# Experts in another order in the first block, and longer runs of weights per partition in the second

## The chip, the cores and the metric

The program runs on one core of a Trainium2 chip, with no other core at work. The metric is device time in microseconds (us) of one execution. Before the change the median of three runs is 2199.96 us, the lowest 2197.1 and the highest 2201.53. A profile comes from one further execution, whose own time is 2198.48 us.

## The reference

Everything is float32: 256 tokens of 1024 features go through two blocks.

The first block is `x + mixer(norm(x))`, then `x + memory_attention(norm(x))`, then `x + hierarchical_moe(norm(x))`. The mixture of experts there has 16 experts in four groups; each token takes two experts of one group:

```python
for e in range(16):
    act = silu(h @ w_gate[e]) * (h @ w_up[e])      # 1024 -> 256
    y = y + combine[:, e:e+1] * (act @ w_down[e])  # 256 -> 1024
```

The second block has two layers over 256 latent tokens and 256 context tokens. The first layer's mixer is a state space scan (SSD) in both directions, the second one's is attention. After each mixer comes an expert-choice mixture, in the first layer for latent and context tokens, in the last layer for latent tokens alone:

```python
gate, idx = top_k(softmax(h @ router_w).T, 32)     # 16 experts, 32 tokens each
xg = h[idx]
y = einsum(silu(xg @ w1[e]) * (xg @ w3[e]), w2[e]) # 1024 -> 1024 -> 1024
out.at[idx].add(y * gate)
```

`w1`, `w3` and `w2` are 4 MB for each expert, so 192 MB for each layer: they are most of what the program reads.

## The kernel before, in words

A tile here is a 128-partition buffer in SBUF. A TensorE instruction multiplies a stationary operand (`lhsT`, loaded by LDWEIGHTS, at most 128 x 128) with a moving one (`rhs`, up to 512 columns) into PSUM. SyncE (SP) issues every weight DMA, in its own program order, and none of them before the tile that it fills is free. A scheduler builds each engine's program from the order in which the Python code emits work and from a simulated timeline, so neighbouring instructions of one engine may come from different places in the code.

**The weight ring.** `ring()` hands out tiles of 128 x 4096 floats (2 MB) from a list of slots in turn: six in the first block's experts, seven in the first layer's of the second block, nine in its last layer's. A tile is refilled when every product that reads it is done.

**First block's experts** (`group_moe`, `group_round`). Tokens are put into expert slots, 64 for an expert, so a pair of experts has 128 rows. The one-hot matrix `oh` gathers: `gather` multiplies the token rows (`hi` and `lo`, two parts of the float32 value; the trace calls `hi` rhi and hT) with it, 32 matmuls for 512 slots, at line 1092, and evicts with the norm's gain `moe_norm_g` into `xg` at 1096 and 1098. `xg` is held as features on partitions: chunk k of eight has features 128k to 128k + 127. Then for each of eight pairs, in the order of the code: `oc` and its transposes (1107, 1111) and `back`, for the scatter; gate and up in one PSUM bank (1124), from two ring tiles, the upper and the lower 512 features of both experts; `act` (1136 to 1138) on ScalarE and VectorE; its transposes (1141) and `actT` (1143); the down product (1158) from one ring tile; `y` (1160, 1161); and the scatter into four accumulators (1165). `gate_order` names the tiles in the order of use; the first six are loaded ahead, while the mixer and the memory attention run.

The weights of that stage are laid out so that partition p has rows p, p + 128, ... of a matrix. A DMA of gate or up (1051) so has runs of 256 floats, 1 KB; one of down (1056) runs of 1024 floats, 4 KB.

**Second block's experts** (`choice_run`, `choice_group`). The first layer has 64 rows for each expert (32 latent, 32 context) and does groups of two experts, eight groups; the last layer has 32 rows and groups of four, four groups. A group does three products, `moe_w1_2`, `moe_w3_2` and `moe_w2_2`, each by `product` (1803): for each quarter q of the 1024 input features it takes one tile for each two experts and multiplies two chunks of features. Here partition p has features 8p to 8p + 7, next to each other in memory; a tile has two of these rows for each of two experts, and its two DMAs (`choice_tile`, 1653) have runs of 2 x 1024 floats, 8 KB. The gather of that stage (1765) already reads its stationary operand with a stride of eight, `v[:, i, k::8]`. A product's scatter is at 1851.

`group_round` is also built for later rounds, for tokens that didn't fit into the 64 slots; these parts are skipped when there are none, as in these runs.

Of the kernel before, what the change touches and what calls it, by code (L numbers as in the profile page):

```python
# [28 lines left out]
P = 128  # L29
D = 1024  # L30
T = 256
# [47 lines left out]
class Net:  # L79
# [861 lines left out]
    def group_moe(self, pool, tile_, late):  # L941
# [5 lines left out]
        nc.vector.tensor_tensor(wr, wr, self.colv("moe_norm_g")[:, :, None].to_broadcast([P, 8, 20]), op=OP.mult)  # L947
        self.hold = wr[:, 0, :1]
# [91 lines left out]
    gate_order = [x for i in range(8) for x in (("gu", i, 0), ("gu", i, 1), ("d", i, 0))]  # L1040

    def group_weights(self, what):

        kind, n, h = what
        a = self.a
        t = self.ring()
        if kind == "gu":
            v = t.rearrange("p (e k c) -> p e k c", e=2, k=4)
            for j in range(2):
                for m, nm in enumerate(("moe_w_gate", "moe_w_up")):  # L1050
                    self.nc.sync.dma_start(v[:, j, :, 256 * m:256 * m + 256],
                                           a[nm][0, 2 * n + j, 512 * h:512 * h + 512].rearrange("(k p) c -> p k c", p=P))
            return v
        v = t.rearrange("p (k c) -> p k c", k=4)
        for j in range(2):
            self.nc.sync.dma_start(v[:, 2 * j:2 * j + 2], a["moe_w_down"][0, 2 * n + j].rearrange("(k p) c -> p k c", p=P))
        return v

    def down_half(self, late, pr, n):

        w = late([P, 4, 512], "y", 2)
        for j in range(2):
            self.nc.sync.dma_start(w[:, 2 * j:2 * j + 2], self.a["moe_w_down"][0, 2 * pr + j][:, n * 512:(n + 1) * 512]
                                   .rearrange("(k p) c -> p k c", p=P))
        return w

    def group_round(self, r, ahead, tile_, late, hi, lo, pos, comb):
# [18 lines left out]
        g = self.colv("moe_norm_g")  # L1086
# [15 lines left out]
        for pr in range(E // 2):  # L1102
            if pr == 2:
                gather(1, "tf")
# [8 lines left out]
            junk = late([P, T], "act", 2)  # L1113
# [4 lines left out]
            if r == 0:  # L1118
                for h in range(2):
                    w = ahead.pop(0) if ahead else self.group_weights(("gu", pr, h))  # L1120
                    for k in range(4 * h, 4 * h + 4):
                        for j in range(2):
                            c0 = (2 * pr + j) * CAP
                            nc.tensor.matmul(gu[j * 64:j * 64 + 64], lhsT=xg[:, k, c0:c0 + CAP], rhs=w[:, j, k % 4],
                                             start=(k == 0), stop=(k == 7))
            else:
                for j in range(2):
                    c0 = (2 * pr + j) * CAP
                    for m, nm in enumerate(("moe_w_gate", "moe_w_up")):
                        w = late([P, 8, 256], "y", 2)  # L1130
                        nc.sync.dma_start(w, self.a[nm][0, 2 * pr + j].rearrange("(k p) c -> p k c", p=P))
# [656 lines left out]
    def choice_group(self, l, grp, EG, S, samples, xg, aff, pos, gr, actT, whole, tile_):  # L1788
# [5 lines left out]
        def product(nm, x):  # L1794
# [3 lines left out]
            for q in range(4):  # L1798
                ws = [self.choice_tile(nm, l, e0 + j, q) for j in range(0, EG, 2)]
                for k in (2 * q, 2 * q + 1):  # L1800
                    for n, p in enumerate(ps):
                        for j in range(EG):
                            nc.tensor.matmul(p[j * S:(j + 1) * S], lhsT=x(k, j),  # L1803
                                             rhs=ws[j // 2][:, j % 2, k % 2, n * 512:(n + 1) * 512],
# [332 lines left out]
```

## Time and profile before

| | |
|---|---|
| median of three runs | 2199.96 us (2197.1 to 2201.53) |
| the profiled execution | 2198.48 us, span of its instructions 2196.7 us |
| mean granted TensorE clock | 0.971 of full speed |
| busy TensorE, VectorE, ScalarE, GpSimd | 1960.7, 968.4, 633.2, 460.3 us |
| bytes moved | 603.53 MB, mean 275 GB/s |
| last of it, first block's experts | about 310 to 452 us |
| second block, first layer's experts | about 1057 to 1519 us |
| second block, last layer's experts | about 1741 to 2197 us |

The profile divides the span in 40 slices of 54.9 us; digits are busy tenths. A busy TensorE is not one at its peak: the ends of matmuls are modelled. The chain of waits goes back from the last instruction, at each step to what released it. The stages are told apart by the lines that run in them.

### The profile page before, as it was taken

How to read it: one execution, taken by the hardware profiler on the slowest of the kernel's cores; microseconds unless marked ns; L12 is line 12 of the kernel's file. 1: busy time of each engine (PE TensorE's matmuls, PEld its weight loads, DVE VectorE, ACT ScalarE, POOL GpSimd, SP SyncE). 2: the span in 40 equal slices, each digit the busy share in tenths (PEclk: the TensorE clock that was granted, in tenths of full speed). 3: DMA queues.
4: the chain of work that ended last, by engine and by line, in shares of the span. 5: the costliest groups of instructions: out<-in, count | busy, mean ns of one | idle time of the engine just before them, and what ended most of it. 6: DMA issues, size and time to landing. Idle time of an engine off the chain costs nothing.

```text
span 2196.7 us, 24031 instructions
## 1 busy us (share of the span) xinstructions
PE 1960.7 (89%) x9107; PEld 1043.9 (48%) x9128; DVE 968.4 (44%) x1643; ACT 633.2 (29%) x1174; POOL 460.3 (21%) x483
## 2 busy tenths in 40 slices
PE   7989879989999999889899999997989688888886
PEld 6667633356767777567333333333756322222211
DVE  6776542159777787666222222212765301010101
ACT  6554422154544555444100000001454200000000
POOL 4440110023233333522011111111753100000000
PEclk9999989999999999999999999999989899999998
DMA  7564949943232321275899999997538799999996
GB/s 243 184 205 135 304 169 346 324 155 107 87 106 69 123 87 54 93 248 205 331 420 419 420 420 419 420 419 311 221 125 312 285 421 420 421 420 421 421 421 280
DMA packets 185785, 603.53 MB, mean 275 GB/s; under 512 B 21555, under 2 KB 94982, under 8 KB 132414
## 3 DMA queue, kind: packets, MB, share of 16 engines
q1 hardware_dynamic: 185662, 601.92, 71.4%
q8 instruction: 74, 1.21, 0.2%
q14 instruction: 49, 0.40, 0.1%
HBM read 597.09 MB, written 4.78 MB: 274 GB/s over the span
## 4 chain that ended last, share of the span: by engine, by line
DMA 37%; PE 13%; DVE 3%; POOL 1%; ACT 1%; issue 1%; POOLq 0%; SPq 0%; DVEq 0%; ACTq 0%
DMA w<-in_moe_w_dram 37%; PE ps L1803 4%; PE ps L1765 1%; PE ps L1288 1%; PE ps L1287 1%; PE ps L1289 1%; PE ps L2024 1%; PE ps L2006 1%; POOL s L235 0%; PE ps L1220 0%; PE ps L1851 0%; PE ps L1698 0%; PE ps L1989 0%; DVE o L1854 0%; PE ps L1990 0%
## 5 line engine op out<-in xcount | busy, mean ns | idle before, releaser
L1803 PE MATMUL ps<-w,xg 128*64 128x512 f32 (+1 forms) x2048 | 497.2, 602 | 52.9 <-DMA w<-in_moe_w_dram 52.6
L1803 PEld LDWEIGHTS ps<-w,xg 128*64 128x64 f32 (+1 forms) x2048 | 142.5, 123 | 374.5 <-issue 242.5
L1855 POOL TENSOR_TENSOR x<-x,o 128x512 f32<-128x512 f32 x24 | 38.7, 1614 | 671.5 <-DVE o L1854 671.5
L1287 PE MATMUL ps<-hT,ws 128*128 128x512 f32 x384 | 156.7, 408 | 4.7 <-DVE ada L1222 4.5
L1288 PE MATMUL ps<-hT,ws 128*128 128x512 f32 x384 | 156.8, 408 | 0.0
L1289 PE MATMUL ps<-hT,ws 128*128 128x512 f32 x384 | 155.0, 404 | 0.0
L1803 PE MATMUL ps<-w,ctx 128*32 128x512 f32 x512 | 128.2, 599 | 23.8 <-DMA w<-in_moe_w_dram 22.7
L1803 PE MATMUL ps<-w,actT 128*64 128x512 f32 x512 | 129.3, 597 | 5.2 <-DMA w<-in_moe_w_dram 3.2
L1845 DVE SCALAR_TENSOR_TENSOR y<-ps,s,y 128x512 fp32r<-128x512 f32 x24 | 18.0, 748 | 261.5 <-ACT y L1844 261.5
L1493 DVE SCALAR_TENSOR_TENSOR conv<-pad,cols,conv 128x512 f32<-128x512 f32 x124 | 112.0, 904 | 2.6 <-ACT conv L1486 0.4
L1844 ACT ACTIVATE y<-ps,s 128x512 fp32r<-128x512 f32 x24 | 16.5, 686 | 327.1 <-PE ps L1803 260.5
L1287 PEld LDWEIGHTS ps<-hT,ws 128*128 128x128 f32 x384 | 72.6, 189 | 26.5 <-DVE ada L1222 5.2
L1803 PEld LDWEIGHTS ps<-w,ctx 128*32 128x32 f32 x512 | 29.2, 108 | 117.7 <-DMA w<-in_moe_w_dram 61.5
L1803 PEld LDWEIGHTS ps<-w,actT 128*64 128x64 f32 x512 | 45.3, 136 | 79.4 <-issue 64.4
L1288 PEld LDWEIGHTS ps<-hT,ws 128*128 128x128 f32 x384 | 72.7, 189 | 18.9 <-issue 3.8
L1289 PEld LDWEIGHTS ps<-hT,ws 128*128 128x128 f32 x384 | 72.6, 189 | 17.9 <-issue 1.9
L1282 DVE TENSOR_TENSOR ws<-wr,ws 128x1024 fp32r<-128x1024 f32 x48 | 62.3, 1299 | 41.3 <-ACT ws L1281 34.7
L1854 DVE TENSOR_TENSOR o<-ps,g 128x512 f32<-128x512 f32 x80 | 51.7, 686 | 62.2 <-PE ps L1851 61.7
L1282 DVE TENSOR_TENSOR ws<-w,ws 128x1024 fp32r<-128x1024 f32 x46 | 62.2, 1357 | 20.3 <-ACT ws L1281 19.9
L1555 POOL TENSOR_TENSOR seg<-seg,seg 128x512 f32<-128x512 f32 x32 | 47.1, 1471 | 114.4 <-ACT seg L1553 99.6
L1553 ACT ACTIVATE seg<-ps 128x512 f32<-128x512 f32 x96 | 54.7, 597 | 49.1 <-PE ps L1548 16.1
L1835 DVE TENSOR_TENSOR ctx<-ctx,ps 128x512 f32<-128x512 f32 x8 | 5.5, 687 | 140.1 <-PE ps L1803 140.1
(639 smaller groups left out, 3690.9 us busy)
## 6 DMA issues: line engine op xcount, KB each, us to landing
w<-in_moe_w_dram SPq DMA_DIRECT2D x384, 1024.0 KB
v<-in_ada_w_dram SPq DMA_DIRECT2D x32, 512.0 KB
w<-in_moe_w_up_dram SPq DMA_DIRECT2D x32, 512.0 KB
w<-in_moe_w_gate_dram SPq DMA_DIRECT2D x32, 512.0 KB
w<-in_moe_w_down_dram SPq DMA_DIRECT2D x16, 1024.0 KB
wr<-in_ssd_in_w_dram SPq DMA_DIRECT2D x16, 1024.0 KB
w<-in_ssd_out_w_dram SPq DMA_DIRECT2D x32, 512.0 KB
w<-in_ada_w_dram SPq DMA_DIRECT2D x8, 2048.0 KB
```

What stands on the lines that cost most here:

```text
L1282: (eng or self.nc.vector).tensor_tensor(lo, x, hi.bitcast(F32), op=OP.subtract)
L1287: t.matmul(p, lhsT=L[0], rhs=R[0], start=start, stop=False, **kw)
L1288: t.matmul(p, lhsT=L[0], rhs=R[1], start=False, stop=False, **kw)
L1289: t.matmul(p, lhsT=L[1], rhs=R[0], start=False, stop=stop, **kw)
L1493: nc.vector.scalar_tensor_tensor(seq(cv), pad[:, :, j:j + 256], tap(j), seq(cv), op0=OP.mult, op1=OP.add)
L1553: nc.scalar.activation(e, p, AF.Exp)
L1555: nc.gpsimd.tensor_tensor(ex[0][0], ex[0][0], ex[1][0], op=OP.add)
L1765: nc.tensor.matmul(p, lhsT=v[:, i, k::8], rhs=oh[:, i].rearrange("p e c -> p (e c)"), start=(j == 0), stop=(j == 3))
L1803: nc.tensor.matmul(p[j * S:(j + 1) * S], lhsT=x(k, j), rhs=ws[j // 2][:, j % 2, k % 2, n * 512:(n + 1) * 512], start=(k == 0), stop=(k == ...
L1854: nc.vector.tensor_tensor(o, q, gr[s][:, c], op=OP.mult)
L1855: (nc.gpsimd if i else nc.vector).tensor_tensor(xx[:, i, c], xx[:, i, c], o, op=OP.add)
L2006: nc.tensor.transpose(t[:, kt], L[:, par, kt * P:(kt + 1) * P], self.ident)
```

## The change

In the first block's experts the loop is split in two functions. `enter(pr)` has everything up to `act`; `leave(pr)` has the transposes of act, the down product and the scatter. `enter` of pair p + 1 now stands ahead of `leave` of pair p, and `gate_order` follows. The weights are laid out as in the second block: partition p has rows 8p to 8p + 7 of gate and up, and rows 2p and 2p + 1 of down, each next to each other in memory; a gate/up tile is one whole expert, with a run of 8 KB for gate and one for up, and down has runs of 8 KB. For that the gather reads `src[:, i, k::8]`, the transposes of act read `act[:, k::2]`, and the norm's gain is loaded a second time, as 8 for each partition (`moe_g`). A buffer of ScalarE's (`junk`) takes its space from another tag.

In the second block a product gets a parameter `nk`, the rows of one expert in a tile: with 2 a tile is as before; with 4 it is one expert's, filled by one DMA of 2 MB with runs of 16 KB. `nk` is 2 in the first and the last product of each layer and in the first layer's second product, and 4 in the other 21 of 24 and 10 of 12 products.

```diff
-    gate_order = [x for i in range(8) for x in (("gu", i, 0), ("gu", i, 1), ("d", i, 0))]
+    gate_order = [("gu", 0, 0), ("gu", 0, 1)] + [
+        x for i in range(8) for x in ([("gu", i + 1, 0), ("gu", i + 1, 1)] if i < 7 else []) + [("d", i, 0)]]
...
-            v = t.rearrange("p (e k c) -> p e k c", e=2, k=4)
-            for j in range(2):
-                for m, nm in enumerate(("moe_w_gate", "moe_w_up")):
-                    self.nc.sync.dma_start(v[:, j, :, 256 * m:256 * m + 256],
-                                           a[nm][0, 2 * n + j, 512 * h:512 * h + 512].rearrange("(k p) c -> p k c", p=P))
+            v = t.rearrange("p (m k c) -> p m k c", m=2, k=8)
+            for m, nm in enumerate(("moe_w_gate", "moe_w_up")):
+                self.nc.sync.dma_start(v[:, m], a[nm][0, 2 * n + j].rearrange("(p k) c -> p k c", k=8))
...
-                    nc.tensor.matmul(p, lhsT=src[:, i, k * P:(k + 1) * P], rhs=oh[:, i, n * 512:(n + 1) * 512],
+                    nc.tensor.matmul(p, lhsT=src[:, i, k::8], rhs=oh[:, i, n * 512:(n + 1) * 512],
...
-                for h in range(2):
-                    w = ahead.pop(0) if ahead else self.group_weights(("gu", pr, h))
-                    for k in range(4 * h, 4 * h + 4):
-                        for j in range(2):
-                            c0 = (2 * pr + j) * CAP
-                            nc.tensor.matmul(gu[j * 64:j * 64 + 64], lhsT=xg[:, k, c0:c0 + CAP], rhs=w[:, j, k % 4],
-                                             start=(k == 0), stop=(k == 7))
+                w = [ahead.pop(0) if ahead else self.group_weights(("gu", pr, j)) for j in range(2)]
+                for k in range(8):
+                    for j in range(2):
+                        c0 = (2 * pr + j) * CAP
+                        nc.tensor.matmul(gu[j * 64:j * 64 + 64].rearrange("p (m c) -> p m c", m=2),
+                                         lhsT=xg[:, k, c0:c0 + CAP], rhs=w[j][:, :, k], start=(k == 0), stop=(k == 7))
...
+            return act, back, ws
+
+        def leave(pr, act, back, ws):
...
-                nc.tensor.transpose(t[:, k], act[:, k * P:(k + 1) * P], self.ident)
+                nc.tensor.transpose(t[:, k], act[:, k::2], self.ident)
...
+        held = enter(0)
+        for pr in range(E // 2):
+            now = held
+            if pr == 2:
+                gather(1, "tf")
+            if pr + 1 < E // 2:
+                held = enter(pr + 1)
+            leave(pr, *now)
...
-    def choice_tile(self, nm, l, e0, q):
-
-        v = self.ring().rearrange("p (e k c) -> p e k c", e=2, k=2)
-        for e in range(2):
+    def choice_tile(self, nm, l, e0, nk, q):
+
+        v = self.ring().rearrange("p (e k c) -> p e k c", k=nk, c=D)
+        for e in range(4 // nk):
             src = self.a[nm][l, e0 + e].rearrange("(p k) c -> p k c", k=8)
-            self.nc.sync.dma_start(v[:, e], src[:, 2 * q:2 * q + 2])
+            self.nc.sync.dma_start(v[:, e], src[:, nk * q:nk * q + nk])
...
-            for q in range(4):
-                ws = [self.choice_tile(nm, l, e0 + j, q) for j in range(0, EG, 2)]
-                for k in (2 * q, 2 * q + 1):
+            ne = 4 // nk
+            for q in range(8 // nk):
+                ws = [self.choice_tile(nm, l, e0 + j, nk, q) for j in range(0, EG, ne)]
+                for k in range(nk * q, nk * q + nk):
...
+        for act, p in zip(acts, product("moe_w1_2", rows, 4 if grp else 2)):
...
+        for n, p in enumerate(product("moe_w3_2", rows, 4 if grp or EG > 2 else 2)):
...
+        for n, p in enumerate(product("moe_w2_2", lambda k, j: actT[:, k, j * S:(j + 1) * S], 4 if e0 + EG < 16 else 2)):
```

TensorE in the middle of the first block's experts, from the end of one pair's gate/up (L1124) over the transposes of act (L1141) and of oc (L1111) and the down product (L1158) to the first scatter (L1165). Before:

```order
L1124 MATMUL ps_6085<-w_6099,xg_5708 64x512 x4
L1141 MATMUL ps_6116<-const,act_6112 128x128 x2
L1111 MATMUL ps_6149<-const,oc_6147 128x128 x2
L1158 MATMUL ps_6125<-w_6121,actT_6119 64x512 x4
L1158 MATMUL ps_6132<-w_6121,actT_6119 64x512 x4
L1165 MATMUL ps_5761<-y_6124,back_6083 128x512
...
L1124 MATMUL ps_6157<-w_6158,xg_5708 64x512 x8
```

The same place now; gate/up is L1124 still, the transposes are L1145 and L1112, the down product L1162 and the scatter L1169:

```order
L1124 MATMUL ps_6108<-w_6112,xg_5702 64x512
L1124 MATMUL ps_6108<-w_6109,xg_5702 64x512
L1124 MATMUL ps_6108<-w_6112,xg_5702 64x512
L1162 MATMUL ps_6144<-w_6140,actT_6138 64x512 x4
L1162 MATMUL ps_6151<-w_6140,actT_6138 64x512 x4
L1145 MATMUL ps_6203<-const,act_6131 128x128 x2
L1112 MATMUL ps_6236<-const,oc_6234 128x128 x2
L1169 MATMUL ps_5755<-y_6143,back_6038 128x512
```

The down product stood behind the transposes of its own pair's act; now it stands ahead of them, and the act (act_6131) that is transposed behind it is the next pair's. Gate/up alternates between two tiles, and both are read to the end.

SP in the same stage, the DMAs for gate/up (L1051) and down (L1056) of a pair behind the first six tiles. Before:

```order
L1051 DMA w_5942<-in_moe_w_gate_dram 128x4x256
L1051 DMA w_5942<-in_moe_w_up_dram 128x4x256
L1051 DMA w_5942<-in_moe_w_gate_dram 128x4x256
L1051 DMA w_5942<-in_moe_w_up_dram 128x4x256
L1051 DMA w_5955<-in_moe_w_gate_dram 128x4x256
L1051 DMA w_5955<-in_moe_w_up_dram 128x4x256
L1051 DMA w_5955<-in_moe_w_gate_dram 128x4x256
L1051 DMA w_5955<-in_moe_w_up_dram 128x4x256
L1056 DMA w_5977<-in_moe_w_down_dram 128x2x1024 x2
L1051 DMA w_6014<-in_moe_w_gate_dram 128x4x256
```

The same now (gate/up L1054, down L1058):

```order
L1054 DMA w_5860<-in_moe_w_gate_dram 128x2048
L1054 DMA w_5860<-in_moe_w_up_dram 128x2048
L1058 DMA w_5888<-in_moe_w_down_dram 128x2048 x2
L1054 DMA w_5973<-in_moe_w_gate_dram 128x2048
L1054 DMA w_5973<-in_moe_w_up_dram 128x2048
L1054 DMA w_5976<-in_moe_w_gate_dram 128x2048
L1054 DMA w_5976<-in_moe_w_up_dram 128x2048
L1058 DMA w_6004<-in_moe_w_down_dram 128x2048 x2
L1054 DMA w_6041<-in_moe_w_gate_dram 128x2048
```

A gate/up tile had four DMAs of 128 x 4 runs of 256 floats; it has two with one run of 2048 floats for each partition. Behind the first gate/up tile there is now a down tile, then two gate/up tiles and a down tile in turn.

TensorE in the last layer of the second block, one product of four experts (ctx is the stationary operand, one for each expert). Before:

```order
L1803 MATMUL ps_15322<-w_15324,ctx 32x512 x2
L1803 MATMUL ps_15323<-w_15324,ctx 32x512 x2
L1821 MATMUL ps_15451<-const,oc_15442 128x128 x2
L1803 MATMUL ps_15322<-w_15327,ctx 32x512
L1803 MATMUL ps_15323<-w_15327,ctx 32x512
L1803 MATMUL ps_15322<-w_15327,ctx 32x512
L1803 MATMUL ps_15323<-w_15327,ctx 32x512
L1803 MATMUL ps_15322<-w_15324,ctx 32x512 x2
L1803 MATMUL ps_15322<-w_15327,ctx 32x512 x2
```

The same now (L1818; L1836 are transposes for the scatter):

```order
L1818 MATMUL ps_14865<-w_14867,ctx 32x512
L1818 MATMUL ps_14866<-w_14867,ctx 32x512
L1836 MATMUL ps_14986<-const,oc_14977 128x128 x2
L1818 MATMUL ps_14865<-w_14869,ctx 32x512
L1818 MATMUL ps_14866<-w_14869,ctx 32x512
L1818 MATMUL ps_14865<-w_14871,ctx 32x512
L1818 MATMUL ps_14866<-w_14871,ctx 32x512
L1818 MATMUL ps_14865<-w_14873,ctx 32x512
L1818 MATMUL ps_14866<-w_14873,ctx 32x512
L1818 MATMUL ps_14865<-w_14867,ctx 32x512
```

Two tiles of two experts each were read, several matmuls of one in a row; now four tiles of one expert each are read side by side, each to its fourth row.

## Rows read from the trace of the kernel before

**Rows 1.** The page: span, busy tenths of TensorE and DMA, bytes, in 40 slices.

```profile
span 2196.7 us, 24031 instructions
...
PE   7989879989999999889899999997989688888886
...
DMA  7564949943232321275899999997538799999996
GB/s 243 184 205 135 304 169 346 324 155 107 87 106 69 123 87 54 93 248 205 331 420 419 420 420 419 420 419 311 221 125 312 285 421 420 421 420 421 421 421 280
```

**Rows 2.** The page: the chain that ended last, by engine and by line.

```profile
DMA 37%; PE 13%; DVE 3%; POOL 1%; ACT 1%; issue 1%; POOLq 0%; SPq 0%; DVEq 0%; ACTq 0%
DMA w<-in_moe_w_dram 37%; PE ps L1803 4%; PE ps L1765 1%; PE ps L1288 1%; PE ps L1287 1%; PE ps L1289 1%; PE ps L2024 1%; PE ps L2006 1%; POOL s L235 0%; PE ps L1220 0%; PE ps L1851 0%; PE ps L1698 0%; PE ps L1989 0%; DVE o L1854 0%; PE ps L1990 0%
```

**Rows 3.** The chain in order of time: start us, us, what.

```profile
1100.17 13.95 PE ps L1803 x64
...
1257.99 19.94 DMA w<-in_moe_w_dram
...
2177.21 2.78 PE ps L1803 x18
```

**Rows 4.** TensorE in order of time, first block: start, us, what, [idle before <-releaser].

```profile
398.02 0.44 PE L1141 MATMUL ps<-const,act 128*128 128x128 f32 x2 [1.40 <-DVE act L1138]
398.94 3.65 PE L1158 MATMUL ps<-w,actT 128*64 128x512 f32 x16 [0.25 <-ACT actT L1143]
...
414.31 3.65 PE L1158 MATMUL ps<-w,actT 128*64 128x512 f32 x16 [0.25 <-ACT actT L1143]
```

**Rows 5.** Waits, 300 to 460 us: engine, what <- releaser: us, times, longest.

```profile
PE ps L1141 <- DVE act L1138: 11.6, 8, 1.8
...
PE ps L1158 <- ACT actT L1143: 2.0, 7, 0.5
```

**Rows 6.** Instructions of the two gathers, by line: ns minimum/median/maximum.

```profile
L1092 PEld LDWEIGHTS ps<-hT,rhi x32: 186/188/330, 310.0 to 357.9; 128*128 128x128 f32 x32
...
L1765 PEld LDWEIGHTS ps<-oh,hi x48: 312/329/342, 1018.9 to 1743.7; 128*128 128x128 f32 x48
```

**Rows 7.** TensorE in order of time where gather matmuls stand among others.

```profile
318.33 0.50 PE L1092 MATMUL ps<-hT,rhi 128*128 128x512 f32 x1
...
319.45 1.08 PE L1124 MATMUL ps<-w,xg 128*64 128x512 f32 x4
...
1730.66 0.63 PE L1765 MATMUL ps<-oh,hi 128*128 128x512 f32 x1
...
1731.96 1.92 PE L1803 MATMUL ps<-w,xg 128*32 128x512 f32 x16
```

**Rows 8.** SP in order of time, first block's experts.

```profile
330.50 1.42 SPq L1051 DMA_DIRECT2D w<-in_moe_w_up_dram  x1
...
388.23 2.11 SPq L1056 DMA_DIRECT2D w<-in_moe_w_down_dram  x2
```

**Rows 9.** Stretches: PE, PEld, DVE, ACT, POOL busy, clock, DMA share, GB/s.

```profile
330.00:335.00 5.00, 4.74 (x23) 1.78 (x21) 1.10 (x3) 2.12 (x5) 0.61 (x1) 1.00 1.09 348
394.00:398.00 4.00, 2.63 (x12) 0.77 (x10) 0.84 (x2) 0.38 (x1) 0.00 (x0) 1.00 1.03 407
1200.00:1250.00 50.00, 48.92 (x200) 19.11 (x197) 14.06 (x27) 4.34 (x8) 7.08 (x5) 1.00 1.01 421
```

**Rows 10.** The page: DMA packets by size; the instruction queue.

```profile
DMA packets 185785, 603.53 MB, mean 275 GB/s; under 512 B 21555, under 2 KB 94982, under 8 KB 132414
...
q8 instruction: 74, 1.21, 0.2%
```

**Rows 11.** TensorE in order of time, last layer of the second block.

```profile
1864.63 1.91 PE L1803 MATMUL ps<-w,xg 128*32 128x512 f32 x4 [0.60 <-DMA w<-in_moe_w_dram]
1867.12 4.39 PE L1803 MATMUL ps<-w,xg 128*32 128x512 f32 x24 [0.59 <-DMA w<-in_moe_w_dram]
```

**Rows 12.** A stretch at that layer's start (columns as in rows 9).

```profile
1760.00:1765.00 5.00, 4.90 (x15) 1.27 (x19) 0.00 (x0) 0.00 (x0) 0.00 (x0) 0.50 1.01 421
```

More of the change, by code (lines that the diff above doesn't have):

```diff
@@ L947, in group_moe @@
         nc.vector.tensor_tensor(wr, wr, self.colv("moe_norm_g")[:, :, None].to_broadcast([P, 8, 20]), op=OP.mult)
+        self.moe_g = tile_([P, 8], "g")
+        nc.sync.dma_start(self.moe_g, a["moe_norm_g"][0].rearrange("(p k) -> p k", k=8))
         self.hold = wr[:, 0, :1]
@@ L1038, in group_moe @@
         self.group_round(0, self.ahead, *env)
-    gate_order = [x for i in range(8) for x in (("gu", i, 0), ("gu", i, 1), ("d", i, 0))]
+    gate_order = [("gu", 0, 0), ("gu", 0, 1)] + [
+        x for i in range(8) for x in ([("gu", i + 1, 0), ("gu", i + 1, 1)] if i < 7 else []) + [("d", i, 0)]]
     def group_weights(self, what):
-        kind, n, h = what
+        kind, n, j = what
         a = self.a
@@ L1055, in group_weights @@
         for j in range(2):
-            self.nc.sync.dma_start(v[:, 2 * j:2 * j + 2], a["moe_w_down"][0, 2 * n + j].rearrange("(k p) c -> p k c", p=P))
+            self.nc.sync.dma_start(v[:, 2 * j:2 * j + 2], a["moe_w_down"][0, 2 * n + j].rearrange("(p k) c -> p k c", k=2))
         return v
@@ L1063, in down_half @@
             self.nc.sync.dma_start(w[:, 2 * j:2 * j + 2], self.a["moe_w_down"][0, 2 * pr + j][:, n * 512:(n + 1) * 512]
-                                   .rearrange("(k p) c -> p k c", p=P))
+                                   .rearrange("(p k) c -> p k c", k=2))
         return w
@@ L1085, in group_round @@
                 nc.vector.tensor_tensor(o, self.c("iota")[:, None, :].to_broadcast([P, E // 2, CAP]), wide(pr_), op=OP.is_equal)
-        g = self.colv("moe_norm_g")
+        g = self.moe_g
         def gather(n, tags):
@@ L1101, in group_round, with enter @@
         acc = [[self.ps(t) for t in "al"] for _ in range(2)]
-        for pr in range(E // 2):
-            if pr == 2:
-                gather(1, "tf")
+        def enter(pr):
             oc = tile_([P, 2, 2, CAP], "oc", 2)
@@ L1112, in group_round @@
             ws = self.st([P, 1])
-            junk = late([P, T], "act", 2)
+            junk = late([P, 2, P], "actT", 2).rearrange("p a q -> p (a q)")
             nc.scalar.activation(junk, t, AF.Copy, scale=0.5, accum_out=ws)
@@ L1130, in group_round @@
                         w = late([P, 8, 256], "y", 2)
[L1131 removed]
+                        nc.sync.dma_start(w, self.a[nm][0, 2 * pr + j].rearrange("(p k) c -> p k c", k=8))
                         for k in range(8):
@@ L1792, in choice_group, with product @@
         e0 = grp * EG
-        def product(nm, x):
+        def product(nm, x, nk=4):
             tag = self.turn("py")
             ps = [self.ps(tag) for _ in range(2)]
-            for q in range(4):
-                ws = [self.choice_tile(nm, l, e0 + j, q) for j in range(0, EG, 2)]
-                for k in (2 * q, 2 * q + 1):
+            ne = 4 // nk
+            for q in range(8 // nk):
+                ws = [self.choice_tile(nm, l, e0 + j, nk, q) for j in range(0, EG, ne)]
+                for k in range(nk * q, nk * q + nk):
                     for n, p in enumerate(ps):
@@ L1829, in choice_group @@
         rows = lambda k, j: xg[:, k, e0 + j].rearrange("p s c -> p (s c)")
-        for act, p in zip(acts, product("moe_w1_2", rows)):
+        for act, p in zip(acts, product("moe_w1_2", rows, 4 if grp else 2)):
             nc.scalar.activation(act, p, AF.Tanh, scale=0.5)
             nc.vector.scalar_tensor_tensor(act, act, 1.0, p, op0=OP.add, op1=OP.mult)
-        for n, p in enumerate(product("moe_w3_2", rows)):
+        for n, p in enumerate(product("moe_w3_2", rows, 4 if grp or EG > 2 else 2)):
             act = acts[n]
@@ L1841, in choice_group @@
             nc.scalar.activation(actT[:, 4 * n:4 * n + 4], t, AF.Copy)
-        for n, p in enumerate(product("moe_w2_2", lambda k, j: actT[:, k, j * S:(j + 1) * S])):
+        for n, p in enumerate(product("moe_w2_2", lambda k, j: actT[:, k, j * S:(j + 1) * S], 4 if e0 + EG < 16 else 2)):
             y = tile_([P, 2, 512], "y", 1, F32R)
```

2 lines of the change are left out of this document (1 added, 1 removed).

## The prediction

> **What bounds the kernel now.** I read the page first: its slices, then the chain of waits, then the chain in order of time, and only then single stages. In the slices [rows 1] two plateaus stand out, slices 21 to 27 and 33 to 39, where the DMA engines are full and move 419 to 421 GB/s. These are the two layers of experts of the second block. The chain of waits [rows 2] says the same: 37% of the span, some 810 us, is DMA into the weight tiles of these layers. In order of time [rows 3] the chain there is one link after another of 19.94 us for eight DMAs of 1 MB, which is 8.39 MB / 19.94 us = 420.7 GB/s. In the same rows TensorE does a whole product of the first layer (64 instructions) in 13.95 us when it has nothing to wait for, and a product's weights take 19.94 us: DMA is the bound, with 6 us to spare on TensorE. At the end DMA stops at 2177.2, and 19.5 us of products, scatter and norm follow.
>
> The first block's experts are another stage. In the steady state a pair of experts takes 15.37 us of TensorE from one down product to the next [rows 4]; in each, TensorE stands 1.40 us before the transposes of act and 0.25 us before the down product. Over the stage these are 11.6 and 2.0 us [rows 5]. No wait of TensorE for a weight DMA of any size is among them: TensorE bounds there, with DMA close behind.
>
> The sum is made against the profiled execution, 2198.5 us (span 2196.7 and 1.8 around it), which is 1.5 us under the median of the runs, 2199.96.
>
> **First block's experts, the order.** Before, TensorE did gate/up of a pair, waited for its act, transposed it, did its down product. Now the down product of pair p stands between gate/up of pair p+1 and the transposes of pair p+1. The down product takes 3.65 us [rows 4], the act chain 1.40 us: the wait is hidden, and likewise the 0.25 us for actT, behind the scatter. The second half of the down product writes the PSUM buffer from which act of p+1 is still read; its first half (1.8 us) covers these 1.40 us. Removed: 11.6 + 2.0 = 13.6 us. If the cover goes, because gate/up weights are late, the same 1.7 us per pair come back.
>
> Added: the gather and the transposes read their stationary operand with a stride. A contiguous load of the gather takes 188 ns, the strided one of the second block 329 ns [rows 6]. Where four gather matmuls stand between expert matmuls they take 319.45 - 318.33 = 1.12 us contiguous, and 1731.96 - 1730.66 = 1.30 us strided [rows 7]: 0.18 us a group, 2.9 us for 16 groups, nothing where loads run under other matmuls. Sixteen transposes of act with 0.14 us more each at most: 2.2 us. Bounds 0 and 5.1, taken 3. The small DMA of the gains goes out with the router's weights, some 20 us before the gather needs it: nothing.
>
> Weights of this stage: SP's rows tell what is in flight [rows 8]: gate and up in runs of 1 KB move 348 GB/s, down in runs of 4 KB 407 [rows 9]. A pair is 4.19 MB and 2.10 MB: 12.0 + 5.2 = 17.2 us of DMA; in runs of 8 KB at 420.7 it is 15.0 us. TensorE needs 15.37 - 1.65 = 13.7 us a pair from now on, so DMA would be next to bind, if six tiles (two pairs) were not loaded ahead. Both gate/up tiles of pair 0 are now freed together, when its gate/up products end and not half-way; from then DMA has 18 tiles of 4.98 us to bring, 90 us, and TensorE still has seven pairs of 13.7, the second gather (32 x 0.28 = 9 us) and a down product with its scatter, some 110 us. DMA ends early and stays hidden. The stage gains 13.6 - 3 = 10.6 by this; I take 9, since the first release comes later and y may be waited for at the end. Bounds: 14 and nothing. What follows up to the second block's experts is TensorE at nine tenths and more [rows 1], so a shift passes through.
>
> **Second block's weights.** Of 24 products of the first layer 21, and of 12 products of the second 10, get runs of 16 KB. At one link of 19.94 us for a product of two experts, and two for one of four, these are 21 x 19.94 + 10 x 39.88 = 817.5 us of DMA. No row has a 16 KB run on this queue. The time of a packet on one of 16 engines (16 x size / rate) is 47.1 ns for 1 KB, 161.0 for 4 KB, 311.5 for 8 KB [rows 3, 9]. Carried on from 4 and 8 KB (37.6 ns per KB) a 16 KB packet takes 612 ns, carried on from 1 and 8 KB 614: 427 to 428 GB/s, 1.5 to 1.7% less time, 12.2 to 13.9 us. I take 12, next to the row of 8 KB. The ends: all of the fixed part gone, 37.8 ns per KB or 434 GB/s, gives 25 us; cut into 8 KB again, 0, against which the instruction queue's 74 packets for 1.21 MB speak, 16 KB each [rows 10]; and, below nothing, a fall back to the 407 of 4 KB would cost 27 us, for which no row speaks, as each longer run here was faster.
>
> The Trainium skill ("DMA: Bandwidth & Descriptors", section "Why small descriptors are slow (HBM only)") gives a packet a fixed cost of about 3 cycles beside one per 32 bytes. By it 16 KB instead of 8 KB saves 3 of 518 cycles, 0.58%, 4.7 us in place of 12. By the same rule and its ceiling of 435 GB/s, runs of 1 KB would move 398 GB/s, and the trace has 348, so it disagrees on the size of the fixed cost.
>
> Tiles are now one expert's: a batch is two of them in the first layer, four in the second, and all come free together. In the second layer TensorE now does the first matmuls of each tile as it lands, and the rest after the fourth. Before, 24 instructions after the last landing took 4.39 us [rows 11]; the 52 now take at most 9.5. Five of nine slots are being filled meanwhile, 5 x 4.98 = 24.9 us of DMA, so SP has something to issue throughout. In the first layer it is two of seven slots, the same five, against 7 us of products. The first product of each layer and the last keep two rows, so start and end stay: no change of the 19.5 us.
>
> Sum: 2198.5 - 9 - 12 = 2177.5; on the scale of the median, 2179.
>
> **Rivals.** (B) Runs of 16 KB move no faster: DMA already stands at 420.7, and from 4 to 8 KB it gained 3% only. For it: no row of this queue above 8 KB. Against: the nearly straight line of the three packet times. Only the order gains: 2191.
> (C) The gain levels off: half or less of 12 us, because the fixed part is smaller at long runs. 2199.96 - 9 - 5 = 2186. It is also where the skill's 3 cycles lead, with its 4.7 us.
> (E) The first block gives nothing: DMA, at 15.0 us a pair against 13.7, takes over early, or the strided loads and the late first release eat the stalls. Against: the count of 90 to 110 us. 2200 - 12 = 2188.
> (D) Slower: TensorE loses its clock in the first layer. It now stands still for a tile's landing between short bursts. After such a stand the granted clock was 0.50 [rows 12], which is 1.2 GHz, and 15 instructions filled 4.9 us. A batch of 7 us has to fit DMA's 9.8. If the first half of each ran at 1.2 GHz it would take 10.5, 42 batches 440 us instead of 419: 21 lost there, 6 and 9 still won: 2206. It decides from a mean clock of 7.0 / 9.8 = 0.71. Against: from 1200 to 1250 TensorE did 200 instructions [rows 9], 43.6 us' worth at 13.95 / 64, so it stood for the rest, and the clock was 1.00; and a TensorE that is late has no gaps.
> The Trainium skill ("TensorE: Matmul & The Clock Gate", section "HAM oscillation — how this bites in real kernels") describes this: a kernel that waits for DMA before each slice starts each at the low clock. Rows 12 agree that a stand lowers it; rows 9 show that short ones did not.
>
> **How the numbers follow.** Forecast 0.62, B 0.11, C 0.10, E 0.08, D 0.09. The forecast's own range is 2168 to 2190: the stage 0 to 14, the runs 8 to 16. To hold 8 of 10 I take 2165 to 2194, which takes in B, C and E and leaves out D and a gain near the upper ends. A measurement of this kernel can tell about 0.2%, 4.4 us, from no change: faster is below 2195.6. D's chance is slower; of B, C and E a part falls within it: faster 0.83, same 0.08, slower 0.09.
>
> **What would show it.** In the profile after: the plateaus' GB/s at 427 or so, links of about 19.65 us for 8.39 MB, and some 21,000 packets fewer of 8 KB and more (512 for each of the 21 products, 1024 for each of the 10); waits of the transposes of act for act near nothing and about 13.7 us a pair; no SP wait between DMAs inside the plateaus. I am wrong if GB/s stays at 421, if TensorE waits for gate/up weights in the first block, if the first layer's plateau shows DMA below full, or if its clock falls below 1.

## The result and the profile after

The changed kernel takes 2186.28 us, median of four runs (2183.75 to 2188.18), where the kernel before takes 2200.74 (four runs, one more than above): a ratio of 0.9927, 95% interval 0.9913 to 0.9941, 14.5 us faster. The forecast was 2179 (2165 to 2194), 21 us faster. The direction held, and the size is two thirds of what was forecast. The profiled execution took 2188.18 us, its span is 10.3 us shorter than that of before.

The page of the changed kernel, the lines that answer to [rows 1, 10], with the granted clock:

```profile
span 2186.4 us, 23839 instructions
...
PE   7989879989999999889799898997989767667666
...
PEclk9999989999999999999899999999899889899989
DMA  7554748853232321275799999997537799999996
GB/s 243 179 191 148 294 171 327 365 166 97 87 107 62 127 92 54 88 237 199 317 428 426 426 427 426 428 427 308 223 126 288 288 428 426 429 427 428 427 425 278
DMA packets 131078, 603.49 MB, mean 276 GB/s; under 512 B 18563, under 2 KB 59222, under 8 KB 92558
```

The two plateaus (slices 21 to 27 and 33 to 39) now move 425 to 429 GB/s in place of 419 to 421, and there are 54,700 packets fewer. In slices 33 to 39, the last layer, TensorE's clock is at eight or nine tenths. The same in two stretches of the plateaus of the changed kernel (columns as in [rows 9]), and below them the second of these stretches before:

```profile
1200.00:1250.00 50.00, 47.10 (x196) 17.88 (x193) 14.15 (x27) 4.34 (x8) 7.08 (x5) 1.00 1.01 427
1800.00:2000.00 200.00, 136.49 (x674) 34.12 (x670) 17.65 (x32) 7.17 (x14) 6.46 (x4) 0.91 1.01 427
```

```profile
1800.00:2000.00 200.00, 170.68 (x672) 41.46 (x671) 17.68 (x32) 7.17 (x14) 6.18 (x4) 1.00 1.01 421
```

427 GB/s in both; in the last layer with a clock of 0.91 for TensorE, where it was 1.00. In the first block's experts, TensorE of the changed kernel in order of time, as in [rows 4]:

```profile
392.06 4.02 PE L1162 MATMUL ps<-w,actT 128*64 128x512 f32 x15
396.02 0.50 PE L1145 MATMUL ps<-const,act 128*128 128x128 f32 x2
...
406.22 4.02 PE L1162 MATMUL ps<-w,actT 128*64 128x512 f32 x15
410.17 0.50 PE L1145 MATMUL ps<-const,act 128*128 128x128 f32 x2
```

From one down product (L1162) to the next it is 14.16 us where it was 15.37, and the transposes of act (L1145) carry no wait in brackets. Of the waits of that stage, against [rows 5], one line is left:

```profile
PE ps L1162 <- ACT actT L1147: 0.3, 1, 0.3
```

At the end nothing changed (chain in order of time, as in [rows 3]):

```profile
2166.69 2.78 PE ps L1818 x18
```

Cut by instructions of TensorE, the stages of before and of the changed kernel in three executions (the other two from the runs e4 and g3 below) are, in us:

| | before | changed | e4 | g3 |
|---|---|---|---|---|
| start to the first gather of the first block's experts | 310.0 | 314.5 | 311.9 | 308.7 |
| first gather to the last scatter: first block's experts | 142.2 | 133.5 | 133.4 | 132.3 |
| to the first expert product of the first layer (SSD) | 605.6 | 608.1 | 607.5 | 606.5 |
| first to last product of the first layer | 464.8 | 460.0 | 460.0 | 460.0 |
| to the first read of keys in the attention | 74.9 | 77.9 | 78.2 | 77.2 |
| to the first expert product of the last layer | 131.2 | 130.7 | 130.8 | 131.0 |
| first to last product of the last layer | 452.0 | 445.6 | 445.5 | 445.7 |
| span | 2196.7 | 2186.4 | 2183.5 | 2177.8 |

The three places that the change edits gain 8.7 to 9.9, 4.8 and 6.4 us. Two stretches that it does not edit are longer: the entry of the attention by 2.3 to 3.3, and the SSD by 0.9 to 2.5. The first stretch scatters by almost 6 us between executions of one kernel.

The granted clock is a part of this. The traces know two levels of it, 1.00 and 0.50, and where it is 0.50 a matmul takes nearly twice as long: in the first gather of before, the same matmuls start every 0.43 us at 0.50 (311 us) and every 0.23 us at 1.00 (315.5 us). "Lost to the clock" is an estimate from each trace: half of the time in which TensorE was at work at 0.50. It serves to compare stages that TensorE bounds.

### The profile page after: what moved, and what is told of

Read it like the earlier page. It is cut to its first block, busy times and chain, and to the rows that moved or that the text cites. A ratio compares the mean times of both kernels' runs of the same rounds, so it can differ in the third digit from the quotient of the medians.

```text
span 2186.4 us, 23839 instructions
## 1 busy us (share of the span) xinstructions
PE 1886.7 (86%) x9107; PEld 1033.4 (47%) x9128; DVE 967.2 (44%) x1643; ACT 634.0 (29%) x1174; POOL 456.7 (21%) x483
## 5 line engine op out<-in xcount | busy, mean ns | idle before, releaser
L1818 PE MATMUL ps<-w,xg 128*64 128x512 f32 (+1 forms) x2048 | 452.8, 638 | 111.0 <-DMA w<-in_moe_w_dram 111.0
L1818 PEld LDWEIGHTS ps<-w,xg 128*64 128x64 f32 (+1 forms) x2048 | 130.6, 127 | 394.2 <-issue 236.0
L1818 PE MATMUL ps<-w,ctx 128*32 128x512 f32 x512 | 107.0, 656 | 36.9 <-DMA w<-in_moe_w_dram 35.9
L1818 PE MATMUL ps<-w,actT 128*64 128x512 f32 x512 | 124.4, 596 | 4.0 <-DMA w<-in_moe_w_dram 2.1
L1302 PEld LDWEIGHTS ps<-hT,ws 128*128 128x128 f32 x384 | 73.4, 191 | 19.1 <-issue 3.8
L1818 PEld LDWEIGHTS ps<-w,ctx 128*32 128x32 f32 x512 | 25.2, 115 | 113.4 <-DMA w<-in_moe_w_dram 58.2
L1818 PEld LDWEIGHTS ps<-w,actT 128*64 128x64 f32 x512 | 43.0, 136 | 74.9 <-issue 66.5
L1850 DVE TENSOR_TENSOR ctx<-ctx,ps 128x512 f32<-128x512 f32 x8 | 5.5, 686 | 141.9 <-PE ps L1818 141.9
```

The source lines that it names most:

```text
L1302: t.matmul(p, lhsT=L[0], rhs=R[1], start=False, stop=False, **kw)
L1818: nc.tensor.matmul(p[j * S:(j + 1) * S], lhsT=x(k, j), rhs=ws[j // ne][:, j % ne, k % nk, n * 512:(n + 1) * 512], start=(k == 0), stop=(k ...
```

## The experiments

Ratios are to runs of the kernel before on the same chip. "Attention" and "SSD" are the fifth and the third row of the table above.

**The second block's part alone, and its tiles without its runs.**

```diff
+            for h in range(0, nk, 2):
+                self.nc.sync.dma_start(v[:, e, h:h + 2], src[:, nk * q + h:nk * q + h + 2])
-            self.nc.sync.dma_start(v[:, e], src[:, nk * q:nk * q + nk])
```

(e2 against e1; e1 has only the second block's half of the change's diff.)

> Only the second block's part of the change: tiles of one expert with runs of 16 KB, first block as before. Theory (run length): a packet of 16 KB takes 614 ns where two of 8 KB take 2 x 313, so the two layers' plateaus move 427 to 428 GB/s and end 7.0 and 6.4 us earlier in themselves; in all about 13 us, 2187 to 2188 by the scale of 2200.7. Rival (the clock gives it back): TensorE's shorter and denser bursts lower its clock in the last layer and delay releases; then 5 us or less, 2195 or more.

> As e1, tiles of one expert with four rows each, but every tile is filled by two DMAs with runs of 8 KB. Theory (run length): packets are those of before, 313 ns, 420 to 421 GB/s; no gain, 2199 to 2202. Rival (the tile's shape): the gain comes from larger and fewer waits of TensorE and SP on tiles, so the time is that of e1, about 2188, at 427 GB/s. Granted clock in the last layer as low as with runs of 16 KB by either.

e1: 0.9969 (0.9956 to 0.9981), 2195.98 us. e2: 1.0004 (0.9991 to 1.0016), 2205.77. Stretches of e1, and then of e2:

```profile
1200.00:1250.00 50.00, 46.84 (x196) 17.83 (x193) 14.15 (x27) 4.34 (x8) 7.08 (x5) 1.00 1.01 428
1800.00:2000.00 200.00, 142.67 (x714) 35.43 (x706) 17.66 (x32) 7.17 (x14) 6.47 (x4) 0.88 1.01 427
```

```profile
1200.00:1250.00 50.00, 47.29 (x195) 17.92 (x193) 12.79 (x25) 3.15 (x6) 7.10 (x5) 1.00 1.01 420
1800.00:2000.00 200.00, 139.48 (x669) 34.68 (x669) 17.95 (x34) 7.17 (x14) 6.16 (x4) 0.87 1.01 421
```

With the same tiles, batches and instructions on TensorE, 16 KB move 427 to 428 GB/s and 8 KB 420 to 421. By the trace's packet records a packet of 8 KB takes 313 ns (e2) and one of 16 KB 614 (e1; medians). So the run length is the cause, and the tile's shape gives nothing. The last layer took 445.5 us in e1 and 452.2 in e2, although TensorE's clock was as low in both (0.88 and 0.87): there the clock costs nothing. But e1 gained only 6.8 us as a whole, half of what the theory said: its attention took 81.3 us in place of 74.9. Its 2195.98 us lie where the rival put them, but not for the rival's reason, since the last layer gained its 6.5.

**The first block's part alone, whole and in pieces.** e3 has the first block's half of the change's diff; f3 the layout with the old loop; f4 the new loop with the old layout.

f3, against e3:

```diff
-            if pr + 1 < E // 2:
-                held = enter(pr + 1)
-            leave(pr, *now)
+            leave(pr, *enter(pr))
```

f4, against e3 (down and the transposes of act likewise):

```diff
-                self.nc.sync.dma_start(v[:, m], a[nm][0, 2 * n + j].rearrange("(p k) c -> p k c", k=8))
+                    self.nc.sync.dma_start(v[:, e, :, 256 * m:256 * m + 256],
+                                           a[nm][0, 2 * n + e, 512 * j:512 * j + 512].rearrange("(k p) c -> p k c", p=P))
...
-                    nc.tensor.matmul(p, lhsT=src[:, i, k::8], rhs=oh[:, i, n * 512:(n + 1) * 512],
+                    nc.tensor.matmul(p, lhsT=src[:, i, k * P:(k + 1) * P], rhs=oh[:, i, n * 512:(n + 1) * 512],
```

> Only the first block's part of the change: order and 8 KB runs, second block as before. Theory (stage gain, partly given back): the experts' stage is some 8.7 us shorter, 133 in place of 142 us; of this 2.3 us are lost at the first layer's first tiles of the second block, where one product's last matmuls stand behind four more gather matmuls and the first slot comes free later; in all 6 us, 2194 to 2195. Rival (the clock's dips in the mixer are the price of this change): the mixer before the stage is 4 to 5 us longer in this profile too, and the whole gains 2 us or less, 2199 or more.

> The kernel before with the first block's new layout alone (runs of 8 KB, strided gather and transposes), gate/up and down in the old order, second block as before. Every later stage has the order of before. Theory: the waits for act (11.6) and actT (2.0) stay, the strided gather adds up to 3 us, TensorE bounds and no weight was waited for: 0 to 4 us slower than before, ratio 1.000 to 1.002. Rival (the DMA of 1 KB runs held the stage up): 3 us or more faster.

> The kernel before with the first block's new order alone: gate/up of the next pair ahead of the down product, weights in runs of 1 KB and 4 KB, contiguous gather. Theory: the stage loses its 13.6 us of waits and adds nothing, and DMA (17.2 us a pair against 13.7, six tiles ahead) just keeps up: 10 to 13 us shorter than 142; the attention has the new order, which costs 7.6 as in the kernels with one part alone; in all 3 to 6 us faster, ratio 0.997 to 0.9985. Rival (DMA binds): the stage waits for gate/up weights and gains under 6 us; in all no faster than before.

e3: 0.9994 (0.9981 to 1.0006). f3: 1.0017 (1.0005 to 1.0030). f4: 0.9987 (0.9976 to 0.9998). The experts' stage took 133.3, 149.5 and 136.8 us, the attention 81.2, 76.8 and 77.9. Waits of f3 in the stage, against [rows 5]:

```profile
PE ps L1144 <- DVE act L1137: 11.8, 8, 1.8
...
PE ps L1161 <- ACT actT L1146: 2.1, 7, 0.5
```

The layout alone removes no wait and costs some: the order is what hides them. Two forecasts missed: e3 gained nothing clear of noise in place of 6 us, and f4's stage came out 5.4 us shorter in place of 10 to 13 (the whole 2.9 faster, 0.4 to 5.3, where 3 to 6 were expected). A part of the stage's differences is the clock. With the estimate of it taken off, the stage takes 139.7 us in each of before, e1 and e2, 141.9 in f3, 132.0 and 132.2 in f4 and g1 (below), and 130.6 to 130.7 in e3 and the three profiles of the changed kernel. So the order gives 7.6 us at like clock, and the layout, which costs 2.2 alone, some 1.5 more on top of it: f4 and g1 have one wait of 1.8 us for act that e3 and the changed kernel have not. f4 and then the changed kernel in the middle of the stage:

```profile
343.00:423.00 80.00, 80.00 (x342) 32.89 (x340) 16.94 (x31) 16.13 (x36) 1.85 (x3) 1.00 1.07 364
```

```profile
343.00:423.00 80.00, 80.00 (x342) 35.10 (x340) 16.08 (x29) 15.45 (x35) 1.85 (x3) 1.00 1.00 412
```

With runs of 1 KB DMA is full (1.07, 364 GB/s) and TensorE does the same 342 instructions, and f4 waits for no weight in the stage: DMA just keeps up, as expected. One down product follows the next as in the changed kernel, here in f4:

```profile
388.68 4.02 PE L1162 MATMUL ps<-w,actT 128*64 128x512 f32 x15
...
402.78 4.02 PE L1162 MATMUL ps<-w,actT 128*64 128x512 f32 x15
```

The mixer ahead of the stage was not the price in e3: its first gather began at 313.1, between the values of the changed kernel. What e3 loses is elsewhere: 2.3 us in the first layer (467.1 for 464.8), 6.3 in the attention, and 4.7 in the SSD (610.3 for 605.6), where 16.7 us are lost to the clock in place of 11.9.

**The changed kernel again.**

> The changed kernel again, unaltered, for a second profile. Theory (chance): the 4.8 us that its first profile lost between 100 and 145 us, in code that the change doesn't touch, are dips of TensorE's clock that fall elsewhere in each execution; this profile has another number of them there, and the offset at 300 us is within 3 us of zero. Rival (systematic): the same dips and plus 4 to 5 us again. Median 2184 to 2188 by either.

> The changed kernel, for a comparison on the same chip. Theory: 2186 to 2188.5; first block's experts 133.5, first layer 460.0, last layer 445.6 us, each within 0.3, since these stages came out so in both profiles; the mixers in between differ by up to 5 us with TensorE's half clock. Rival: stages differ as much as the mixers do.

e4: 0.9930 (0.9912 to 0.9948), 2188.11. g3: 0.9919 (0.9905 to 0.9932), 2184.57. The offset of the first gather to that of before was +4.5, +1.9 and -1.2 us: chance. A stretch of the first mixer, in the first profile and in g3:

```profile
115.00:120.00 5.00, 3.92 (x18) 3.63 (x19) 4.94 (x8) 0.17 (x1) 5.00 (x5) 0.56 0.10 15
```

```profile
115.00:120.00 5.00, 3.37 (x30) 2.56 (x29) 4.62 (x8) 1.16 (x3) 5.00 (x6) 1.00 0.22 58
```

The same code ran at a clock of 0.56 and 18 instructions here, and at 1.00 and 30 there. The first and the last layer repeat within 0.1 us, as expected; the experts' stage came out 1.2 us shorter in g3 and missed its 0.3 (1.5 us lost to the clock there, 3.0 and 2.8 in the other two), and g3's median lies 1.4 us under its forecast.

**Code that the change does not touch.** The scheduler's simulated timeline saw other weights at other times, and put instructions of later stages in another order. Two places cost time. At the first layer's start DMA pauses until the first tile of weights is read to its end. DMA from 1040 to 1075 us, forty columns of 0.875 us, before, after, and in h1:

```profile
DMA  9999999999999999400000000000087999999999
GB/s 431 440 431 421 440 412 421 431 440 412 431 403 421 431 412 431 178 0 0 9 0 0 19 0 0 0 0 0 0 140 318 431 403 421 421 449 384 412 431 421
```

```profile
DMA  9999999999999950000000000000037999999999
GB/s 421 431 431 431 440 403 431 421 412 440 403 421 421 421 215 0 0 0 0 19 0 0 0 0 0 0 0 0 0 75 159 346 440 412 440 440 496 431 393 449
```

```profile
DMA  9999999999997000000000000989999989998999
GB/s 440 421 440 431 393 431 440 412 440 375 431 440 309 28 0 0 0 19 0 0 0 0 0 0 9 215 337 412 412 431 421 459 356 449 393 487 356 468 393 449
```

Before, twelve columns are at 30 GB/s or less; after, fourteen, though TensorE's first product came 1.7 us earlier: its last product with that tile now stands behind four more gather matmuls. In h1, twelve again, it doesn't:

```diff
-            if k % 2:
+            if k % 2 == 0:
                 nc.scalar.activation(xg[:, k, :, s], pv, AF.Identity, scale=m[:, k:k + 1], bias=sh[:, k:k + 1])
```

> The changed kernel with the evictions of the second block's gather swapped between ScalarE and VectorE (even chunks on ScalarE). By the instruction order no gather group stands between the last matmuls of the first layer's first tile any more, as in the kernel before; the rest of TensorE's order in attention is that of the changed kernel. Theory: the first slot comes free 2.3 us earlier, DMA's pause at the first layer's start is as long as before, and the first layer takes 457.5 to 458 us in place of 460.0; in all 1.5 to 3 us faster than the changed kernel's 2184.6 to 2188.1. Rival (the pause is set by something else, such as the packets of 16 KB): 460 again.

The first layer took 458.0 us, as the theory said, so the late slot is the cause of these 2.0 us. The whole did not gain: 0.9925 (0.9907 to 0.9943); the attention took 80.6. f2 delays the slot further, by a first product of four rows (`4 if grp or EG == 2 else 2` for `4 if grp else 2`):

> The changed kernel with runs of 16 KB in the first layer's first product too. By the instruction order it has the transposes of kr ahead of the second ada group again, and no gather group between the last matmuls of the first tile; but a first tile of four rows is only read to its end behind two more gather groups. Theory: attention 3 to 4.4 us better than in the changed kernel, the first slot's release some 5 to 6 us later than there (two groups of 4 gather matmuls and 8 products, about 2 x 3.2 us), nothing for one more product at 16 KB (0.3 us); in all 2188 to 2191. Rival (a later release costs nothing, since other slots are free): 2183.5 to 2185.

0.9950 (0.9936 to 0.9964), 2192.77: the first product came 47.4 us behind the first gather of the second block in place of 38.7, though that gather began 4 to 6 us earlier in the stretch; the SSD stretch took 611.0, 2.9 to 4.5 us more than in the changed kernel, and the first layer 463.8, 3.8 more. The four rows cost more than was expected, and the rival falls.

The other place is the entry of the attention. There TensorE transposes kr, the keys, for latent and for context tokens (L1906 before, L1922 after, L1920 in e3); VectorE makes kB from the first result, and the second group of transposes waits for that. The ada products (L1220, L1234) belong to another computation and need neither. Before, after and in e3:

```profile
1577.55 1.03 PE L1906 MATMUL ps<-const,kr 128*128 128x128 f32 x8
...
1581.02 1.92 PE L1220 MATMUL ps<-w,silu_c 128*32 128x512 f32 x16
...
1582.87 1.16 PE L1906 MATMUL ps<-const,kr 128*128 128x128 f32 x8
```

```profile
1570.66 1.93 PE L1234 MATMUL ps<-w,silu_c 128*32 128x512 f32 x16
...
1575.41 1.03 PE L1922 MATMUL ps<-const,kr 128*128 128x128 f32 x8
...
1580.73 1.25 PE L1922 MATMUL ps<-const,kr 128*128 128x128 f32 x8 [1.77 <-DVE kB L1978]
```

```profile
1579.69 1.93 PE L1234 MATMUL ps<-w,silu_c 128*32 128x512 f32 x16
...
1581.54 1.09 PE L1920 MATMUL ps<-const,kr 128*128 128x128 f32 x8
...
1588.99 1.97 PE L1920 MATMUL ps<-const,kr 128*128 128x128 f32 x8 [3.83 <-DVE kB L1976]
```

Before, a group of ada products stands between the two groups of kr and covers the wait for kB. Now it stands ahead of both, and TensorE waits 1.8 us; in e3 3.8, because VectorE's ws, ahead of kB in its program, there takes 3.42 us beside two of GpSimd's, and 1.21 in the changed kernel (VectorE of e3, GpSimd of e3, VectorE of the changed kernel):

```profile
1581.42 3.42 DVE L1296 TENSOR_TENSOR ws<-w,ws 128x1024 fp32r<-128x1024 f32 x1
```

```profile
1578.28 5.47 POOL L1296 TENSOR_TENSOR ws<-w,ws 128x1024 fp32r<-128x1024 f32 x2
```

```profile
1575.12 1.21 DVE L1296 TENSOR_TENSOR ws<-w,ws 128x1024 fp32r<-128x1024 f32 x1
```

f1 moves an ada call by hand:

```diff
             queries(0)()
-            self.ada_two()
             turn = queries(1)
+            self.ada_two()
```

> The changed kernel with one call moved in the last layer's attention: a pair of ada products is emitted behind the second half of the queries in place of ahead of it. TensorE's order then has the transposes of kr ahead of the second group of ada products, as before the change. Theory (untouched code was put in another order): the 4.4 us that the attention loses between the end of the first layer's experts and the first read of qkv (its wait for kB among them) come back but for some 1.5; median 2183.5 to 2185.5 where the changed kernel had 2188.1. Rival (chance or the clock alone): the attention loses 4 us again, median 2187 to 2189.

0.9915 (0.9899 to 0.9931), 2185.64; the attention took 78.9, and the wait for kB was 1.7. The theory in this form fell: kr stood ahead of the ada group again, but still no group between its two halves. Its time is no different from that of the changed kernel, whose interval it shares. All kernels by this wait fall in three classes, whose times in the attention do not overlap. Beside the times stand all of TensorE's waits in that stretch and what it lost to the clock (us, in the order of the kernels):

| wait for kB | kernels | attention | all waits | lost to the clock |
|---|---|---|---|---|
| none | before, e2, f2, f3 | 74.9, 76.5, 76.5, 76.8 | 10.0, 10.0, 9.2, 9.4 | 3.9, 5.7, 3.7, 7.0 |
| 1.7 to 1.8 | changed, e4, g3, f1, f4, g1 | 77.9, 78.2, 77.2, 78.9, 77.9, 77.3 | 10.3, 10.3, 10.9, 10.2, 10.2, 9.9 | 7.0, 7.1, 5.4, 7.0, 7.0, 7.1 |
| 3.8 | e1, e3, g2, h1 | 81.3, 81.2, 81.0, 80.6 | 12.4, 12.2, 12.2, 13.2 | 8.5, 8.6, 8.4, 6.5 |

The third class waits 2 to 4 us more than the first. From the first to the second the waits grow by less than 1 us on the mean, since before, e2 and f3 wait 1.2 us for qT later on, which the second class does not; the rest goes with the clock. f3 lost as much to the clock without the wait for kB, so that the new order lowers the clock is not shown.

**All but the layout, and the last products.** g1 is f4 with the second block's part; g2 has `4` for `4 if e0 + EG < 16 else 2`.

> The whole change but for the first block's new layout: its new order with weights in runs of 1 KB and 4 KB and a contiguous gather, and the second block's runs of 16 KB. By the instruction order the first layer's first tile is read to its end without a gather group in between, as before. Theory (terms add up): stage 5.5 to 7.5 us shorter than 142.2 (8.8 with the layout), first layer 7.0 shorter (4.8 in the changed kernel, whose first slot came 2.3 later), last layer 6.4, attention 1 to 3 longer; in all as fast as the changed kernel within 3 us, so the layout is worth nothing. Rival (the layout carries the first block's gain): 5 us or more slower than the changed kernel.

> The changed kernel with runs of 16 KB in the last product of each layer too. Theory: after the last landing TensorE now has the rest of a batch of four-row tiles to do: in the last layer up to 52 instructions, 7 to 9 us, in place of 18 in 2.8; in the first layer 28 or so in place of 14, 3 us more; the faster packets give back 0.3 and 0.7. In all 5 to 8 us slower than the changed kernel, 2192 to 2196. Rival (the tiles land one by one, and only the last one's instructions are left at the end): within 2 us of it.

g1: 0.9943 (0.9929 to 0.9956), 2191.07, 6.5 us over g3 (the two intervals touch). Its stages are as in the theory (133.8, 457.8 without the late slot, 445.6), yet it is slower, so the theory falls on the whole, and the rival's number came without the rival's reason: in g1's profile the first gather began at 316.9 us (308.7 to 314.5 in the changed kernel) and the SSD took 611.9 (606.5 to 608.1). In the SSD g1 lost 17.0 us to the clock and f4 19.6, the changed kernel 10.4 to 14.7; h1, which has the new layout, lost 18.1. So the layout is worth 0.3 to 1.5 us in its own stage; that it is worth more elsewhere is not shown. g2: 0.9964 (0.9950 to 0.9978), 2195.56, 11 us over g3 and more than the 5 to 8 expected. The last instructions behind the last landing:

```profile
2169.28 6.21 PE ps L1818 x50
```

50 in 6.21 us for 18 in 2.78; the last layer took 448.5 (+2.9), the first 463.1 (+3.1), and the attention fell in the third class (+3.2).

## Why the forecast was right in its direction and too large

**The runs of 16 KB: right.** Forecast 12 us, from the straight line through three packet times at 612 to 614 ns. The packets take 614; the last layer gains 6.4, and the first 6.8 to 7.0 where its first slot is in time (h1, g1): 13.3. B and C are out. An estimate from the Trainium skill ("DMA: Bandwidth & Descriptors", "Why small descriptors are slow (HBM only)"), from its 3 cycles for a packet, gave 4.7; the packets disagree, as the row of 1 KB did. One sign did not come, and told nothing: SP does wait inside the plateaus, 351 us from 1100 to 1500 for TensorE to free tiles, where it waited 303 us for DMA before; DMA was full all the same.

**The first block's order: right in size, in part by luck.** Forecast 9, measured 8.7 to 9.9, and 9.0 with the clock taken off. The waits are gone but for 0.3 us (11.6 and 2.0 before), as forecast. But a pair takes 14.2, not 13.7, and the strided loads that were given 3 us are not why: in f4, without them, it takes 14.1. By the estimate TensorE's work in the stage grew by 4.3 us, where 4.6 had been taken off the 13.6 for other reasons; what lengthens it in the new order was not looked into. The layout alone costs 2.2 us in the stage by the estimate, and 3.7 (1.1 to 6.6, f3) in all. No weight is waited for; E is out.

**D, the clock: its sign came, its price did not.** It was forecast for the first layer, whose mean clock is still 0.98 to 0.99 in the three profiles; it came in the last, where TensorE is at 0.91 (0.87 in e2). DMA bounds there, and e2's last layer is as long as that of before. The Trainium skill ("TensorE: Matmul & The Clock Gate", "HAM oscillation — how this bites in real kernels") describes a kernel that waits for DMA and then starts at the low clock; the trace agrees in part, since the clock was low for some of the time only, and no time hangs on it.

**The step that failed** is "What follows up to the second block's experts is TensorE at nine tenths and more [rows 1], so a shift passes through", with "so start and end stay"; the attention has no term at all. It took code that the diff does not edit as unmoved. The scheduler moved it. At the first slot this cost 2.0 to 2.2 us, as h1 shows (the changed kernel against h1 and g1, e3 against f4; e1, which has the slot in time, took 459.4 for a reason not looked into). In the attention the changed kernel is 1.6 us longer (77.8, the mean of three, against 76.2, the mean of the four kernels without the wait), of which 0.8 is waiting (10.5 against 9.7); the rest goes with the clock, and that the order causes it is not shown. With both the sum is -9.1 - 13.3 + 2.1 + 0.8 = -19.5, where the three comparisons gave -14.5, -15.3 (e4) and -19.1 us (g3); the last one's interval, -20.9 to -15.0, holds it, and the other two end at -19.1 and -19.4. What is left, up to 5 us, stays open: the mixers scatter by as much from one execution to the next, and whether the SSD's +0.9 to +2.5 is part of the change was not separated from the clock. That e1 and e3 together give 8 us and both at once 15 fits the attention: each alone lands in the third class (+6.3), both together in the second.

The forecast's own range, 2168 to 2190, was added up on the scale of the profiled execution; on that of the median it is 2170 to 2192. Either holds the 2186.

## What to carry to other kernels

When a scheduler orders the program by a simulated timeline, a change of DMA shapes or of one loop can reorder stages far behind it. Compare the order of every stage, on every engine and above all where a wait is just covered, before a shift is said to pass through; and expect single edits not to add up. Before a stage's difference between two profiles is put down to an edit, compare the granted clock in it: the first block's experts took 132 to 150 us here, and the estimate of the clock brings kernels with the same code in that stage within 0.3 us of each other. Longer runs pay where DMA is full, but a larger tile is released later: the first and the last product want small ones.

## What was not expected of the hardware

From 8 to 16 KB the packet's time again grew less than its size, 614 ns against 2 x 313. It was forecast, but no row had shown it on this queue. In a DMA-bound layer TensorE's mean clock fell from 1.00 to between 0.87 and 0.91 with tiles that come free in fours, with no effect on the time. And one VectorE operation of 128 x 1024 took 3.42 us in place of 1.21 while GpSimd did the same kind beside it; of the 118 such operations (ws) in e3, the 78 beside which GpSimd did nothing took 1.23 us at most.
